# Rotary embedding: one GpSimd product per tile over a signed sine table, instead of two half products

## The chip, the cores and the metric

The kernel runs on one core of one Trainium2 chip. The metric is device time in microseconds (us) of one execution. All data is float32.

## The reference: what is computed

A rotary position embedding on `x` of shape (8, 2048, 8, 64): batch, position, head, head element. `cos` and `sin` have shape (2048, 32).

```python
x1 = x[..., : x.shape[-1] // 2]
x2 = x[..., x.shape[-1] // 2 :]
cos = cos[None, :, None, :]
sin = sin[None, :, None, :]
out1 = x1 * cos - x2 * sin
out2 = x1 * sin + x2 * cos
return np.concatenate([out1, out2], axis=-1)
```

Each row of 64 elements is two halves of 32. The output row is `x * (cos, cos)` plus the row with its halves exchanged times `(-sin, sin)`. Input and output are 33.55 MB each.

## The kernel before, in words

**Tiling.** The 2048 positions are split over 128 partitions, 16 positions to a partition. A batch is then 8192 elements per partition (16 positions x 8 heads x 64), 4 MB in all, and it has one buffer `xt` in SBUF. There are five of these (`NBUF`). The loop over the 8 batches cuts each into pieces: four of 2048 elements (4 positions), but in batch 0 the first piece, and in batch 7 the last, is cut into two of 1024. So there are 30 pieces of 2048 and 4 of 1024. `rotate` computes one piece in place in `xt`.

**Loads and stores.** Loads are issued on the SP queue (L67), the first five batches at once, the tables behind the first quarter of batch 0. Batches 5 to 7 are loaded after batches 0 to 2 have been stored, since they take over their buffers. Stores are issued on ScalarE's queue (L74). Batch 0 goes out in five parts and batch 7 in three (4096, 2048 and 2048 elements per partition), the others whole, each after its last piece.

**The three kinds of piece.** `t1` holds `x * cos`, `t2` the exchanged row times the signed sine.

- Kind A, 29 of the 34 pieces: GpSimd makes `t2` in two products (L121): the second halves of `t2` from the first halves of `x` times `sin_sb`, then the first halves of `t2` from the second halves of `x` times `nsin`, the negated sine. VectorE makes `t1` in one product against the cosine table in PSUM (L128) and adds both into `xt` (L135). Here `t1` is in PSUM, in a pool of one buffer.
- Kind B, the first pieces of batches 2, 4 and 5: GpSimd and VectorE make `t2` and `t1` as before, but the sum is made on TensorE, as two products with the identity (L140, L141), and ScalarE copies it from PSUM into `xt` (L142).
- Kind C, the first pieces of batches 1 and 3: VectorE makes both products (L128, L145), TensorE adds them with `eye` and `neye`, ScalarE copies (L161). GpSimd has no part.

`t2` of GpSimd rotates through three buffers (`t2_pool`). In kinds B and C, `t1`, and in C `t2` too, lie in `t1s_pool`, two buffers in SBUF.

**Order.** Almost every instruction is wrapped in `keep`, so each engine runs them in the order in which the program states them. The framework adds the semaphores. GpSimd runs its products piece after piece; a new product waits until a buffer of `t2` is free, that is, until the add three pieces earlier is done.

**Tables before the loop.** ScalarE makes `nsin` (L89), copies sine to PSUM (L90) and negates the identity (L91). VectorE copies cosine to PSUM (L92).

Of the kernel before, what the change touches and what calls it, by code (L numbers as in the profile page):

```python
# [9 lines left out]
@with_exitstack  # L10
def kernel(
    ctx: ExitStack,
    tc: tile.TileContext,
    x: bass.AP,
    cos: bass.AP,
    sin: bass.AP,
    out: bass.AP,
):
    nc = tc.nc
    keep = tc.keep_in_program_order  # L20
    f32 = mybir.dt.float32
    PSUM = bass.MemoryType.PSUM

    B, S, H, D = x.shape
    Dh = D // 2
    P = 128
    HD = H * D
    R = S // P
    ROW = R * HD
    UNIT = 4 * HD  # L30
    NBUF = 5
    C = 512
    last = B - 1

    xv = x.rearrange("b (q r) h d -> b q (r h d)", q=P)
    ov = out.rearrange("b (q r) h d -> b q (r h d)", q=P)
    cos_src = cos.rearrange("(q r) d -> q r d", q=P)
    sin_src = sin.rearrange("(q r) d -> q r d", q=P)

    const_pool = ctx.enter_context(tc.tile_pool(name="const", bufs=1))  # L40
    tab_pool = ctx.enter_context(tc.tile_pool(name="tab", bufs=1, space=PSUM))
    t1_pool = ctx.enter_context(tc.tile_pool(name="t1p", bufs=1, space=PSUM))
    o_pool = ctx.enter_context(tc.tile_pool(name="op", bufs=2, space=PSUM))
    t1s_pool = ctx.enter_context(tc.tile_pool(name="t1s", bufs=2))
    xpool = ctx.enter_context(tc.tile_pool(name="xpool", bufs=NBUF))
    t2_pool = ctx.enter_context(tc.tile_pool(name="t2p", bufs=3))

    cos_sb = const_pool.tile([P, R, Dh], f32, tag="cb")
    sin_sb = const_pool.tile([P, R, Dh], f32, tag="sb")
    nsin = const_pool.tile([P, R, Dh], f32, tag="ns")  # L50
    eye = const_pool.tile([P, P], f32, tag="eye")
    neye = const_pool.tile([P, P], f32, tag="neye")
    cos_ps = tab_pool.tile([P, R, Dh], f32, tag="cp")
    sin_ps = tab_pool.tile([P, R, Dh], f32, tag="sp")

    xts = {}

    def spans(sizes):
        lo = 0
        for n in sizes:  # L60
            yield lo, n
            lo += n

    def load(b):
        xt = xpool.tile([P, ROW], f32, tag="xt", name=f"xt{b}")
        for lo, n in spans([UNIT, UNIT, 2 * UNIT] if b == 0 else [ROW]):
            keep(nc.sync.dma_start(out=xt[:, lo : lo + n], in_=xv[b, :, lo : lo + n]))  # L67
            if b == 0 and lo == 0:
                keep(nc.sync.dma_start(out=cos_sb, in_=cos_src))  # L69
                keep(nc.sync.dma_start(out=sin_sb, in_=sin_src))  # L70
        xts[b] = xt

    def store(b, lo, n):
        keep(nc.scalar.dma_start(out=ov[b, :, lo : lo + n], in_=xts[b][:, lo : lo + n]))  # L74

    for b in range(NBUF):
        load(b)

    nc.gpsimd.memset(eye, 0.0)  # L79
    nc.gpsimd.affine_select(  # L80
        out=eye,
        in_=eye,
        compare_op=mybir.AluOpType.not_equal,
        fill=1.0,
        base=0,
        pattern=[[-1, P]],
        channel_multiplier=1,
    )
    keep(nc.scalar.mul(nsin, sin_sb, -1.0))  # L89
    keep(nc.scalar.copy(sin_ps, sin_sb))  # L90
    keep(nc.scalar.mul(neye, eye, -1.0))  # L91
    keep(nc.vector.tensor_copy(cos_ps, cos_sb))  # L92

    def rep(a, n):
        return dataclasses.replace(a, ap=[a.ap[0][:], a.ap[1][:], [0, n], a.ap[-1][:]])

    kinds = {}
    for b, kind in ((1, "C"), (2, "B"), (3, "C"), (4, "B"), (5, "B")):
        kinds[(b, 0)] = kind

    def rotate(b, lo, n):
        kind = kinds.get((b, lo), "A")
        xt = xts[b][:, lo : lo + n]
        r0 = lo // HD
        nr = n // HD
        xk = xt.rearrange("p (r k d) -> p r k d", r=nr, d=Dh)
        xu = xt.rearrange("p (g u d) -> p g u d", u=2, d=Dh)
        if kind == "A":
            t1 = t1_pool.tile([P, n], f32, tag="t1")
        else:  # L110
            t1 = t1s_pool.tile([P, n], f32, tag="t1s")
        if kind == "C":
            t2 = t1s_pool.tile([P, n], f32, tag="t1s")
        else:
            t2 = t2_pool.tile([P, n], f32, tag="t2")
        t1u = t1.rearrange("p (g u d) -> p g u d", u=2, d=Dh)
        t2u = t2.rearrange("p (g u d) -> p g u d", u=2, d=Dh)
        if kind != "C":
            for u, tab in ((1, sin_sb), (0, nsin)):
                keep(  # L120
                    nc.gpsimd.tensor_mul(  # L121
                        out=t2u[:, :, u, :].rearrange("p (r h) d -> p r h d", h=H),
                        in0=xu[:, :, 1 - u, :].rearrange("p (r h) d -> p r h d", h=H),
                        in1=rep(tab[:, r0 : r0 + nr, :], H),
                    )
                )
        keep(
            nc.vector.tensor_mul(  # L128
                out=t1.rearrange("p (r k d) -> p r k d", r=nr, d=Dh),
                in0=xk,  # L130
                in1=rep(cos_ps[:, r0 : r0 + nr, :], 2 * H),
            )
        )
        if kind == "A":
            keep(nc.vector.tensor_add(out=xt, in0=t1, in1=t2))  # L135
        elif kind == "B":
            for j in range(n // C):
                o = o_pool.tile([P, C], f32, tag="o")
                cs = slice(j * C, (j + 1) * C)
                nc.tensor.matmul(o, eye, t1[:, cs], start=True, stop=False)  # L140
                nc.tensor.matmul(o, eye, t2[:, cs], start=False, stop=True)  # L141
                keep(nc.scalar.copy(xt[:, cs], o))  # L142
        else:
            keep(
                nc.vector.tensor_mul(  # L145
                    out=t2.rearrange("p (r k d) -> p r k d", r=nr, d=Dh),
                    in0=xk,
                    in1=rep(sin_ps[:, r0 : r0 + nr, :], 2 * H),
                )
            )  # L150
            G = C // Dh
            for u in range(2):
                for j in range(n // 2 // C):
                    o = o_pool.tile([P, C], f32, tag="o")
                    gs = slice(j * G, (j + 1) * G)
                    nc.tensor.matmul(o, eye, t1u[:, gs, u, :], start=True, stop=False)  # L156
                    nc.tensor.matmul(  # L157
                        o, eye if u else neye, t2u[:, gs, 1 - u, :], start=False, stop=True
                    )
                    keep(  # L160
                        nc.scalar.copy(  # L161
                            xu[:, gs, u, :], o.rearrange("p (g d) -> p g d", d=Dh)
                        )
                    )

    def pieces(b):
        if b == 0:
            return [2 * HD, 2 * HD, UNIT, UNIT, UNIT]
        if b == last:
            return [UNIT, UNIT, UNIT, 2 * HD, 2 * HD]  # L170
        return [UNIT] * 4

    for b in range(B):
        done = 0
        outs = list(spans([2 * UNIT, UNIT, UNIT] if b == last else [ROW]))
        for lo, n in spans(pieces(b)):
            rotate(b, lo, n)
            done = lo + n
            while outs and sum(outs[0]) <= done:
                whole = outs.pop(0)  # L180
                if b == 0:
                    for part in spans([HD, HD, 2 * HD, UNIT, 2 * UNIT]):
                        store(b, *part)
                else:
                    store(b, *whole)
        if b + NBUF <= last:
            load(b + NBUF)
# [30 lines left out]
```

## Time and profile before

| | |
|---|---|
| median of 6 runs | 163.62 us (163.49 to 165.58) |
| the profiled execution | 163.56 us |
| its span, first to last instruction | 161.8 us |
| GpSimd (POOL) busy | 138.9 us, 86% |
| VectorE (DVE) busy | 140.1 us, 87% |
| TensorE (PE) busy | 45.5 us, 28% |
| ScalarE (ACT) busy | 14.4 us, 9% |
| read from HBM, written | 34.08 MB, 33.55 MB |
| mean rate of the DMA engines over the span | 418 GB/s |

The profile is one execution as the hardware profiler took it. Its page cuts the span into 40 equal slices; in the rows of an engine each digit is its busy share in tenths. A row of the trace's timeline has the start from the span's begin, the duration, the engine, the line of the kernel, the operation, and what is written and read, with `t` for every temporary, whichever pool it is from; in square brackets stands how long the engine had been idle and what ended that. The chain of waits is found from the last instruction backwards: at each step to what released it. Durations of GpSimd instructions overlap their neighbours by some hundredths of a us, so their cost is better taken from start to start.

### The profile page before, as it was taken

The numbers are of one execution on the slowest core, as the hardware profiler recorded it, in microseconds if no ns is written. First come the engines' busy times: TensorE is split into PE (matmuls) and PEld (weight loads), VectorE is DVE, ScalarE is ACT, GpSimd is POOL, SyncE is SP. The second block draws the span as 40 slices with busy tenths as digits, with TensorE's granted clock in tenths as the row PEclk, the third lists the DMA queues.
The fourth block names the chain that finished last, engine by engine and source line by source line (L and its number), as shares of the span: only waits on it lengthen the run. The fifth ranks groups of instructions, "written<-read, shape, count | busy, mean of one in ns | idle before, by whom it ended". The sixth has DMA issues, their size and how long they took to land.

```text
span 161.8 us, 470 instructions
## 1 busy us (share of the span) xinstructions
PE 45.5 (28%) x80; PEld 18.3 (11%) x80; DVE 140.1 (87%) x66; ACT 14.4 (9%) x24; POOL 138.9 (86%) x70
## 2 busy tenths in 40 slices
PE   0000000499008930894039802990000000000000
PEld 0000000143003400341014201430000000000000
DVE  0468999999999999999999999999999999999600
ACT  3300000013100410022001400130000000000000
POOL 1299999999999899999994999999999999996000
PEclk9999999999965997589857995699555555555555
DMA  5999999999998989998999999999999999999995
GB/s 192 407 442 473 471 413 413 413 421 438 438 470 348 462 357 454 429 478 389 429 470 397 438 456 405 446 446 407 438 446 413 438 454 405 446 446 405 417 407 213
DMA packets 3746, 67.65 MB, mean 418 GB/s; under 512 B 416, under 2 KB 416, under 8 KB 1056
## 3 DMA queue, kind: packets, MB, share of 16 engines
q1 hardware_dynamic: 1728, 34.08, 49.7%
q10 hardware_dynamic: 2016, 33.56, 48.3%
q14 instruction: 2, 0.02, 0.0%
HBM read 34.08 MB, written 33.55 MB: 418 GB/s over the span
## 4 chain that ended last, share of the span: by engine, by line
DVE 75%; POOL 9%; issue 6%; DMA 3%; SPq 0%; DVEq 0%; POOLq 0%
DVE t L128 40%; DVE xt L135 33%; POOL t L121 9%; DMA sin_sb<-in_sin_dram 3%; DVE t L145 3%; DVEq L135 0%; SPq L69 0%; SPq L67 0%; POOLq L121 0%
## 5 line engine op out<-in xcount | busy, mean ns | idle before, releaser
L121 POOL TENSOR_TENSOR t<-xt,sin_sb 128x1024 f32<-128x1024 f32 (+1 forms) x32 | 70.4, 2200 | 8.7 <-DMA sin_sb<-in_sin_dram 5.6
L128 DVE TENSOR_TENSOR t<-xt,cos_ps 128x2048 f32<-128x2048 f32 (+1 forms) x34 | 73.4, 2167 | 0.8
L121 POOL TENSOR_TENSOR t<-xt,nsin 128x1024 f32<-128x1024 f32 (+1 forms) x32 | 70.5, 2202 | 0.0
L135 DVE TENSOR_TENSOR xt<-t,t 128x2048 f32<-128x2048 f32 (+1 forms) x29 | 62.2, 2145 | 5.4 <-POOL t L121 2.5
L140 PE MATMUL o<-t,eye 128*128 128x512 f32 x24 | 15.5, 733 | 25.4 <-DVE t L128 25.4
L156 PE MATMUL o<-t,eye 128*128 128x512 f32 x16 | 11.4, 821 | 37.9 <-DVE t L128 37.9
L141 PE MATMUL o<-t,eye 128*128 128x512 f32 x24 | 14.6, 695 | 0.0
L142 ACT COPY xt<-o 128x512 f32<-128x512 f32 x12 | 7.0, 586 | 44.8 <-PE o L141 44.8
L140 PEld LDWEIGHTS o<-t,eye 128*128 128x128 f32 x24 | 5.5, 246 | 33.5 <-issue 33.5
L161 ACT COPY xt<-o 128x512 f32<-128x512 f32 x8 | 4.7, 586 | 44.8 <-DVE t L128 26.6
L156 PEld LDWEIGHTS o<-t,eye 128*128 128x128 f32 x16 | 3.8, 257 | 42.8 <-POOL t L121 30.5
L141 PEld LDWEIGHTS o<-t,eye 128*128 128x128 f32 x24 | 5.4, 227 | 7.4 <-issue 7.4
L92 DVE COPY cos_ps<-cos_sb 128x512 f32<-128x512 f32 x1 | 0.7, 695 | 6.1 <-DMA cos_sb<-in_cos_dram 6.1
L157 PE MATMUL o<-t,neye 128*128 128x512 f32 x8 | 5.4, 780 | 0.1
L145 DVE TENSOR_TENSOR t<-xt,sin_ps 128x2048 f32<-128x2048 f32 x2 | 4.6, 2282 | 0.0
L157 PE MATMUL o<-t,eye 128*128 128x512 f32 x8 | 4.1, 592 | 0.0
L157 PEld LDWEIGHTS o<-t,neye 128*128 128x128 f32 x8 | 2.0, 262 | 4.2 <-issue 4.2
L157 PEld LDWEIGHTS o<-t,eye 128*128 128x128 f32 x8 | 1.5, 190 | 1.9 <-issue 1.9
L89 ACT ACT_TABLE_LOAD x1 | 1.3, 1283 | 0.7 <-PEq L202 0.7
L89 ACT ACTIVATE nsin<-sin_sb 128x512 f32<-128x512 f32 x1 | 0.6, 630 | 4.8 <-DMA sin_sb<-in_sin_dram 4.8
L90 ACT COPY sin_ps<-sin_sb 128x512 f32<-128x512 f32 x1 | 0.6, 579 | 0.0
L79 POOL MEMSET eye<- 128x128 f32 x1 | 0.2, 204 | 0.3 <-POOLq L202 0.3
(6 smaller groups left out, 1.0 us busy)
## 6 DMA issues: line engine op xcount, KB each, us to landing
xt<-in_x_dram SPq DMA_DIRECT2D x7, 4096.0 KB, 27.4
out_dram<-xt ACTq DMA_DIRECT2D x6, 4096.0 KB, 33.3
out_dram<-xt ACTq DMA_DIRECT2D x2, 2048.0 KB, 24.3
out_dram<-xt ACTq DMA_DIRECT2D x3, 1024.0 KB, 11.1
xt<-in_x_dram SPq DMA_DIRECT2D x2, 1024.0 KB, 6.0
xt<-in_x_dram SPq DMA_DIRECT2D x1, 2048.0 KB, 11.4
out_dram<-xt ACTq DMA_DIRECT2D x2, 256.0 KB, 19.0
out_dram<-xt ACTq DMA_DIRECT2D x1, 512.0 KB, 32.6
```

The lines of the kernel that those rows point to most:

```text
L89: keep(nc.scalar.mul(nsin, sin_sb, -1.0))
L92: keep(nc.vector.tensor_copy(cos_ps, cos_sb))
L121: nc.gpsimd.tensor_mul(out=t2u[:, :, u, :].rearrange("p (r h) d -> p r h d", h=H), in0=xu[:, :, 1 - u, :].rearrange("p (r h) d -> p r h d" ...
L128: nc.vector.tensor_mul(out=t1.rearrange("p (r k d) -> p r k d", r=nr, d=Dh), in0=xk, in1=rep(cos_ps[:, r0 : r0 + nr, :], 2 * H),)
L135: keep(nc.vector.tensor_add(out=xt, in0=t1, in1=t2))
L140: nc.tensor.matmul(o, eye, t1[:, cs], start=True, stop=False)
L141: nc.tensor.matmul(o, eye, t2[:, cs], start=False, stop=True)
L142: keep(nc.scalar.copy(xt[:, cs], o))
L145: nc.vector.tensor_mul(out=t2.rearrange("p (r k d) -> p r k d", r=nr, d=Dh), in0=xk, in1=rep(sin_ps[:, r0 : r0 + nr, :], 2 * H),)
L156: nc.tensor.matmul(o, eye, t1u[:, gs, u, :], start=True, stop=False)
L157: nc.tensor.matmul(o, eye if u else neye, t2u[:, gs, 1 - u, :], start=False, stop=True)
L161: nc.scalar.copy(xu[:, gs, u, :], o.rearrange("p (g d) -> p g d", d=Dh))
```

## The change

GpSimd's two products per piece become one over the whole piece. Its input is `x` with the two halves of each row exchanged: the pattern `swapped` starts at element 32 of a row, steps back by 32 to the other half, and on by 64 to the next row. Its table `sgn` holds for each position a negated and a plain sine row side by side, read by `signed` once for each of the 8 heads. The output is the piece of `t2` in one run. `nsin` goes.

`sgn` is made on ScalarE with four instructions, for positions 0 to 3 and then 4 to 15, ahead of the copy of sine to PSUM. The sine and cosine tables in SBUF lose their own places and lie in the two buffers of `t1s_pool`, which the first piece of kind C takes over later.

```diff
-    cos_sb = const_pool.tile([P, R, Dh], f32, tag="cb")
-    sin_sb = const_pool.tile([P, R, Dh], f32, tag="sb")
-    nsin = const_pool.tile([P, R, Dh], f32, tag="ns")
+    cos_sb = t1s_pool.tile([P, R, Dh], f32, tag="t1s", name="cos_sb")
+    sin_sb = t1s_pool.tile([P, R, Dh], f32, tag="t1s", name="sin_sb")
+    sgn = const_pool.tile([P, R, 2, Dh], f32, tag="sg")
...
-    keep(nc.scalar.mul(nsin, sin_sb, -1.0))
+    for lo, hi in ((0, 4), (4, R)):
+        keep(nc.scalar.mul(sgn[:, lo:hi, 0, :], sin_sb[:, lo:hi, :], -1.0))
+        keep(nc.scalar.copy(sgn[:, lo:hi, 1, :], sin_sb[:, lo:hi, :]))
     keep(nc.scalar.copy(sin_ps, sin_sb))
     keep(nc.scalar.mul(neye, eye, -1.0))
     keep(nc.vector.tensor_copy(cos_ps, cos_sb))
...
+    def swapped(a, nr):
+        return dataclasses.replace(
+            a,
+            offset=a.offset + Dh,
+            ap=[a.ap[0][:], [HD, nr], [D, H], [-Dh, 2], [1, Dh]],
+        )
+
+    def signed(a, nr):
+        return dataclasses.replace(
+            a, ap=[a.ap[0][:], [D, nr], [0, H], [Dh, 2], [1, Dh]]
+        )
...
         if kind != "C":
-            for u, tab in ((1, sin_sb), (0, nsin)):
-                keep(
-                    nc.gpsimd.tensor_mul(
-                        out=t2u[:, :, u, :].rearrange("p (r h) d -> p r h d", h=H),
-                        in0=xu[:, :, 1 - u, :].rearrange("p (r h) d -> p r h d", h=H),
-                        in1=rep(tab[:, r0 : r0 + nr, :], H),
-                    )
+            keep(
+                nc.gpsimd.tensor_mul(
+                    out=t2.rearrange("p (r h u d) -> p r h u d", r=nr, h=H, u=2),
+                    in0=swapped(xt, nr),
+                    in1=signed(sgn[:, r0 : r0 + nr, :, :], nr),
                 )
+            )
```

## The prediction

> **What bounds the kernel now.** I read the page first for the share of each engine, then its DMA lines, then the chain that ended last, and then asked the trace for stretches of time near the end.
>
> The page gives three resources that are nearly full: VectorE (DVE) is busy 87% of the span, GpSimd (POOL) 86%, and the DMA engines almost all of it. The DMA lines of the page:
>
> ```profile
> DMA  5999999999998989998999999999999999999995
> GB/s 192 407 442 473 471 413 413 413 421 438 438 470 348 462 357 454 429 478 389 429 470 397 438 456 405 446 446 407 438 446 413 438 454 405 446 446 405 417 407 213
> q1 hardware_dynamic: 1728, 34.08, 49.7%
> q10 hardware_dynamic: 2016, 33.56, 48.3%
> ```
>
> q1 carries the loads and q10 the stores; together their packets take 98.0% of 16 engines' span. Only the first and the last slice are half empty. The stretches of the trace (columns: stretch, length, busy time of PE, PEld, DVE, ACT, POOL, clock, DMA share, GB/s) say the same of the end:
>
> ```profile
> 5.00:20.00 15.00, 0.00 (x0) 0.00 (x0) 11.44 (x8) 1.35 (x3) 13.07 (x8) 1.00 1.04 441
> 120.00:140.00 20.00, 0.00 (x0) 0.00 (x0) 19.35 (x9) 0.00 (x0) 20.00 (x10) 0.50 0.98 424
> 140.00:152.00 12.00, 0.00 (x0) 0.00 (x0) 11.48 (x8) 0.00 (x0) 8.25 (x6) 0.50 1.00 430
> 158.00:160.00 2.00, 0.00 (x0) 0.00 (x0) 0.00 (x0) 0.00 (x0) 0.00 (x0) 0.50 0.86 365
> 160.00:161.80 1.80, 0.00 (x0) 0.00 (x0) 0.00 (x0) 0.00 (x0) 0.00 (x0) 0.50 0.02 9
> ```
>
> The DMA share stays near 1.0 until 159 us, though the last arithmetic ends at 152.5. So the chain of waits, which puts the end down to VectorE, has to be read with care:
>
> ```profile
> DVE 75%; POOL 9%; issue 6%; DMA 3%; SPq 0%; DVEq 0%; POOLq 0%
> ```
>
> That chain follows the last store back to the add that released it. It does not show that this store then stood behind others. The timeline of ScalarE's queue shows the last store issued at 152.51, the DMA lines from there on give its time to landing, and the DMA lines from the start to 152.5 what the store queue had moved by then:
>
> ```profile
> 152.51 0.34 ACTq L74 DMA_DIRECT2D out_dram<-xt  x1
> ...
> out_dram<-xt ACTq DMA_DIRECT2D x1, 1024.0 KB, 8.3
> ...
> q10 hardware_dynamic: 1655, 30.52, 46.6%
> ```
>
> All stores are 33.56 MB and the last is 1.05 MB, so 32.51 MB were issued before it; 32.51 - 30.52 = 1.99 MB were still waiting, which is 4.7 us at 427 GB/s (67.65 MB over about 158.3 us in which packets moved). The same subtraction gives 3.1 MB at the store of 147.3, 3.0 MB at that of 142.6 and 2.95 MB at that of 133.0. The store queue is never dry in the last 30 us, and before that both queues hold work. My reading: transfers set the end, and VectorE and GpSimd run a few us ahead of what they must. The shortest landing of any 1 MB transfer in the trace is 4.7 us (the first load), so the last store could be issued about 8.3 - 4.7 = 3.6 us later before the end moves: an estimate.
>
> Below that bound, VectorE and GpSimd race each other. The timelines of both in the second half (start, duration):
>
> ```profile
> 102.20 2.34 POOL L121 TENSOR_TENSOR t<-xt,sin_sb 128x1024 f32<-128x1024 f32 x1
> 104.50 2.36 POOL L121 TENSOR_TENSOR t<-xt,nsin 128x1024 f32<-128x1024 f32 x1
> 106.80 2.36 POOL L121 TENSOR_TENSOR t<-xt,sin_sb 128x1024 f32<-128x1024 f32 x1
> ...
> 143.35 1.26 POOL L121 TENSOR_TENSOR t<-xt,sin_sb 128x512 f32<-128x512 f32 x1
> 144.56 1.26 POOL L121 TENSOR_TENSOR t<-xt,nsin 128x512 f32<-128x512 f32 x1
> ...
> 102.28 2.29 DVE L135 TENSOR_TENSOR xt<-t,t 128x2048 f32<-128x2048 f32 x1 [0.33 <-POOL t L121]
> 104.61 2.29 DVE L128 TENSOR_TENSOR t<-xt,cos_ps 128x2048 f32<-128x2048 f32 x1
> 107.00 2.29 DVE L135 TENSOR_TENSOR xt<-t,t 128x2048 f32<-128x2048 f32 x1
> ```
>
> Start to start, a GpSimd pair takes 4.57 to 4.60 us and a VectorE pair of an A tile 4.72 us. VectorE is the slower one there; over the whole kernel it waits only 2.5 us for GpSimd, in three places:
>
> ```profile
> DVE xt L135 <- POOL t L121: 2.5, 3, 1.3
> ```
>
> **What the Trainium skill says.** "GPSIMD Engine Reference", section 3.1, gives 4497 ns for a two-input fp32 GpSimd instruction of 2048 elements. The trace agrees with the rate: its pair, 2 x 1024 elements in runs of 32, takes 4.57 us, so runs of 32 cost no more than the page's figure. Section 7 of that page charges about 50% more for reads whose element step exceeds 8 bytes. The innermost step stays one element here, so I don't apply it; nothing in the trace tests a step that goes back. "SBUF — State Buffer", section "SBUF: two separate sides", says that engines and DMA cannot slow each other, and that GpSimd shares one port pair with VectorE instructions that have two SBUF inputs. Here each VectorE product takes its table from PSUM (L128, L145), and each add takes t1 from PSUM, so there is one SBUF input at most; the trace agrees, with VectorE's 2.29 us unvarying beside busy GpSimd. "DMA: Bandwidth & Descriptors", section "Where 436 GB/s comes from", gives 435 GB/s as the ceiling of the port side and 358 as that of HBM. The trace's 427 GB/s is past the second and near the first; at 435 the same bytes would need 155.5 us, 2.8 us less than now.
>
> **The change, part by part.**
>
> GpSimd's products. Of 64 instructions 32 go. Cost per instruction from start-to-start times: 1024 elements 2.28, 512 elements 1.21, so 2.09 ns an element and 0.14 us fixed. A product of 2048 elements is then 0.14 + 2048 x 0.00209 = 4.42 us, one of 1024 is 2.28. Saved: about 0.15 us in each of 28 whole tiles and 0.14 in each of 4 half tiles, 4.8 us of GpSimd time together. None of it lies on the transfers' path. On VectorE's path lie only the waits of 2.5 us, and the next limit there is VectorE's own 4.72 us per tile. The unknown is the read that goes back by 32 elements once in 64. The address pattern has the same three levels as the sine operand had before, so I take no extra cost: 4.42. The ends: 4.35, since the output is now one contiguous run and the fixed part cannot go below nothing by much, and 6.6 if the page's 50% applied anyway.
>
> The tables. One ScalarE product of 512 columns (0.63) becomes two products and two copies, of 128 and of 384 columns. The 128-column row (neye, 0.30) bounds the first two: between 0.15 and 0.30 each, I take 0.27. Sine lands at 6.8, so GpSimd starts at about 7.4 instead of 6.92, 0.45 later (0.25 to 0.6). It waits for both halves, where before its first product needed only sine itself. The second pair and sin_ps and neye end near 9.2 instead of 8.2; their first users are at 11.8 (third tile), 30.3 and about 34, so they are hidden.
>
> The start then goes: first tile's product ready at 7.4 + 2.28 = 9.7 (before 9.4), second 12.0 (12.0), third 16.4 (16.4), fourth 20.9 (20.97). VectorE's first two adds are late by up to 0.35, the third by nothing. Stores of those tiles are issued that much later, while the loads alone keep the DMA engines full (share 1.04 from 5 to 20 us). Cost nothing; uncovered it would be 0.35.
>
> The wait of 0.33 at 102.28 goes (two products sooner, 0.30). VectorE then ends at 152.2 instead of 152.5, GpSimd near 145.
>
> Cosine and sine in the t1s buffers. Their next users are the C products of batch 1 at 28.1 and 30.3; the last readers of the tables end by 9.2. No wait, nothing moved on any queue. The DMA lists and their order are unchanged.
>
> Sum: the transfers' path changes by 0 (down to -0.3 if the last store's earlier issue counts). The profiled execution is 163.56 with a span of 161.8, 1.76 outside it; its own time is 0.06 below the median of 163.62. I take 163.5.
>
> **The rivals.**
>
> Rival 1, the engines set the end after all. For it: the chain is 75% VectorE. Against: the 1.99 MB waiting. It would give 0.25 for VectorE's end (163.3), and at the very most all of the 2.5 us of waits for GpSimd (161.1); only the upper part is faster by 1%. The first two waits, 1.34 and 0.84, are at the start, where GpSimd begins later, so that part is hardly to be had.
>
> Rival 2, slower: reading backwards costs GpSimd extra. For it: no row of the trace has such a read, and GpSimd has little room. Decision point: GpSimd may end 2.9 us later (VectorE's last add ends 4.24 us after GpSimd's end, and must follow it by 1.35) plus 3.6 us of store slack, so 154.7; (154.7 - 7.4 - 0.3) / 30 tile equivalents = 4.90 us per product. Above 0.48 us extra a tile, 15 ns for each of 32 backward steps, the kernel slows by 30 us for each us. At 25 ns a step (an assumed size) a product takes 5.22, GpSimd ends at 164.3, the last add at 165.6, its store lands 4.7 later and the span ends 1.0 after that: 171.3, and 173.1 as a time. Against it: three-level patterns already run at the page's rate.
>
> Rival 3, GpSimd sees no saving, because the fixed part is not paid once but hidden in the pitch. Then nothing moves but the start: 163.6, same as before.
>
> **How the numbers follow.** Transfers set the end and little moves: 0.71 with rival 3 in it, own range 163.0 to 164.3. Rival 2: 0.22. Rival 1 with over 1% gain, or transfers that run nearer 435 GB/s: 0.07. About 1% is what a measurement of this kernel tells from no change. Faster 0.07, same 0.71, slower 0.22. The range goes from 162.0 to 168.5: it leaves out most of rival 1's upper part (0.06) and the part of rival 2 with over 20 ns a step (0.14).
>
> **What would show it.** Right: products at a pitch near 4.42 us, GpSimd starting near 7.4 and waiting more for VectorE, VectorE ending near 152.2, DMA share still 98%, and over 1.5 MB of stores waiting when the last is issued. Wrong: a product over 4.9 us with VectorE waiting for GpSimd in every tile (rival 2), or an end that moves with VectorE's last add by more than 0.3 us (rival 1).

## The result and the profile after

The changed kernel takes 164.70 us (median of 28 runs), the kernel before beside it 163.92 (63 runs). The ratio is 1.0038, 95% interval 1.0019 to 1.0056: slower by 0.6 us, small but clear of no change. The ratio is taken over the fast runs alone, here and in the table below; the medians of all runs lie 0.8 us apart. The forecast was 163.5 us, a little faster than before.

The profiled execution of the changed kernel is one of its longer ones, 165.66 us with a span of 163.7, so the lines below show the effect larger than the median has it. Its page, the DMA lines:

```profile
DMA  5999999999999899999999999999999999999991
GB/s 190 424 446 491 408 410 407 452 440 432 398 432 474 340 422 492 360 456 440 384 456 424 432 450 400 448 440 408 456 424 432 448 400 440 456 400 416 414 422 52
q1 hardware_dynamic: 1728, 34.08, 49.1%
q10 hardware_dynamic: 2016, 33.56, 48.0%
```

The transfers still fill the span up to its last slice. That last slice is where the time is: 52 GB/s. The stretches of the trace at the end (columns as in the prediction):

```profile
120.00:140.00 20.00, 0.00 (x0) 0.00 (x0) 19.35 (x9) 0.00 (x0) 20.00 (x6) 0.50 0.98 424
140.00:152.00 12.00, 0.00 (x0) 0.00 (x0) 11.48 (x8) 0.00 (x0) 7.55 (x3) 0.50 1.00 431
158.00:160.00 2.00, 0.00 (x0) 0.00 (x0) 0.00 (x0) 0.00 (x0) 0.00 (x0) 0.50 0.88 373
160.00:162.00 2.00, 0.00 (x0) 0.00 (x0) 0.00 (x0) 0.00 (x0) 0.00 (x0) 0.50 0.16 66
```

From 120 to 160 us the rates are those of before. Between 160 and 162 us a DMA share of 0.16 remains, two or three of sixteen engines; before, these 2 us had 0.02. The sixteen completion times of the last store say it too: before, all lie between 159.8 and 160.8 us; after, thirteen lie between 159.8 and 160.6, and three at 161.5, 162.8 and 162.8. So most DMA engines end when they ended before, and three of them late (taking one completion time for each engine).

The store queue was not waiting for VectorE. ScalarE's timeline, the DMA lines from the last store's issue on, and those up to it:

```profile
152.91 0.34 ACTq L74 DMA_DIRECT2D out_dram<-xt  x1
...
out_dram<-xt ACTq DMA_DIRECT2D x1, 1024.0 KB, 9.9
...
q10 hardware_dynamic: 1658, 30.57, 46.8%
```

Before that store 32.51 - 30.57 = 1.94 MB were waiting (before: 1.99).

On the engines themselves the change did what it says. The group of whole products, GpSimd's timeline from 98 us on, the add that had waited 0.33 us before, and the waits between the two:

```profile
L134 POOL TENSOR_TENSOR t<-xt,sgn 128x2048 f32<-128x2048 f32 x28 | 125.8, 4521 | 5.2 <-DVE xt L148 5.2
...
98.12 49.42 POOL L134 TENSOR_TENSOR t<-xt,sgn 128x2048 f32<-128x2048 f32 x12 [0.21 <-DVE xt L148]
...
102.68 2.29 DVE L148 TENSOR_TENSOR xt<-t,t 128x2048 f32<-128x2048 f32 x1 [0.23 <-POOL t L134]
...
POOL t L134 <- DVE xt L148: 5.2, 8, 2.3
DVE xt L148 <- POOL t L134: 2.5, 3, 1.7
```

Where neither waits, a whole product starts 4.46 to 4.51 us after the one before it, mostly 4.47 to 4.48 (two halves: 4.57 to 4.60). So about 0.10 us are saved, and GpSimd returns most of that by waiting longer for VectorE, 5.2 us instead of 2.7.

**Where it comes from.** Three places in the trace differ before the end. The first is the first store. The DMA lines of the stretch from 14.0 to 15.45 us, before and then after (queue, packets, MB, share):

```profile
q1 hardware_dynamic: 16, 0.52, 83.7%
q10 hardware_dynamic: 16, 0.03, 5.8%
```

```profile
q1 hardware_dynamic: 16, 0.52, 83.7%
q10 hardware_dynamic: 13, 0.03, 4.7%
```

Each of the sixteen engines moves one load row of 32 KB here, and behind it one store row of 2 KB; the next pair follows 1.29 us later. Before, all sixteen have a store row in this slot. After, three have none and start one slot later. The store was issued at 10.69 us before and at 10.98 after.

The second is the load of batch 4. The text ahead of the prediction counts it among five loads issued at once, but the trace has it much later. The SP queue's timeline, before and then after:

```profile
35.03 0.33 SPq L67 DMA_DIRECT2D xt<-in_x_dram  x1
```

```profile
35.72 0.33 SPq L67 DMA_DIRECT2D xt<-in_x_dram  x1
```

The last of the sixteen completions of the second store, which runs behind the first, comes at 35.01 us before and at 35.71 after. In every trace here but that without the work of the pieces, this load is issued 0.01 to 0.02 us after that moment. So the load takes over the lateness of the last engine, 0.7 us.

The third is the time in which loads start again beside stores of whole batches, from 60 to 80 us; before and then after:

```profile
60.00:80.00 20.00, 9.37 (x16) 3.67 (x16) 19.52 (x10) 2.34 (x4) 19.88 (x10) 0.83 1.04 446
```

```profile
60.00:80.00 20.00, 9.06 (x16) 3.64 (x16) 19.52 (x10) 2.34 (x4) 19.60 (x5) 0.81 1.03 433
```

13 GB/s less over 20 us are 0.26 MB, 0.6 us at the mean rate of 427 GB/s. That resembles the loss between the medians, but it does not account for this execution, whose span is 1.9 us longer. Over the whole stretch from 5 to 158 us the rates are 430 GB/s before and 429 after. What differs is how evenly the DMA engines run: the sixteen completion times of the load of batch 5 spread over 2.0 us before (85.9 to 88.0) and over 3.6 us after (85.9 to 89.5), and those of the last store over 1.0 and 3.0 us.

### The profile page after: what moved, and what is told of

It is laid out like the page before. It is cut to its first block, busy times and chain, and to the rows that moved or that the text cites. A ratio compares the mean times of both kernels' runs of the same rounds, so it can differ in the third digit from the quotient of the medians.

```text
span 163.7 us, 443 instructions
## 1 busy us (share of the span) xinstructions
PE 45.5 (28%) x80; PEld 18.4 (11%) x80; DVE 140.1 (86%) x66; ACT 15.0 (9%) x27; POOL 135.7 (83%) x38
## 4 chain that ended last, share of the span: by engine, by line
DVE 73%; POOL 8%; issue 8%; DMA 3%; SPq 0%; DVEq 0%; ACT 0%
DVE t L141 39%; DVE xt L148 31%; POOL t L134 8%; DMA sin_sb<-in_sin_dram 3%; DVE t L158 3%; DVEq L148 0%; SPq L69 0%; SPq L67 0%; ACT sgn L91 0%; ACT sgn L90 0%
## 5 line engine op out<-in xcount | busy, mean ns | idle before, releaser
L134 POOL TENSOR_TENSOR t<-xt,sgn 128x2048 f32<-128x2048 f32 (+1 forms) x32 | 135.0, 4249 | 11.2 <-ACT sgn L91 6.0
L90 ACT ACTIVATE sgn<-sin_sb 128x128 f32<-128x128 f32 (+1 forms) x2 | 0.8, 413 | 4.8 <-DMA sin_sb<-in_sin_dram 4.8
L91 ACT COPY sgn<-sin_sb 128x128 f32<-128x128 f32 (+1 forms) x2 | 0.8, 387 | 0.0
```

The lines of the kernel that those rows point to most:

```text
L90: keep(nc.scalar.mul(sgn[:, lo:hi, 0, :], sin_sb[:, lo:hi, :], -1.0))
L91: keep(nc.scalar.copy(sgn[:, lo:hi, 1, :], sin_sb[:, lo:hi, :]))
L134: nc.gpsimd.tensor_mul(out=t2.rearrange("p (r h u d) -> p r h u d", r=nr, h=H, u=2), in0=swapped(xt, nr), in1=signed(sgn[:, r0 : r0 + nr, ...
```

## The experiments

The theory, A: the late start of GpSimd shifts the first store by 0.3 us, some DMA engines take its first row one load row later, and the transfers run less well afterwards. Its rivals are B, VectorE's later end moves the end; C, the tiles' new places in SBUF; D, the merged product itself.

All runs in one table. The columns between the name and the ratio are read from the profile of one execution, whose time is given too: issue of the first store, how many of the sixteen engines have a store row between 14.0 and 15.45 us, issue of the load of batch 4, and the rate from 60 to 80 us. The first load lands at 5.4 to 5.7 us of these traces, so times of issue compare to about 0.3 us.

| kernel | first store, us | of 16 | load of batch 4, us | GB/s | profiled, us | ratio to before (95%) |
|---|---|---|---|---|---|---|
| before | 10.69 | 16 | 35.03 | 446 | 163.56 | 1 |
| changed | 10.98 | 13 | 35.72 | 433 | 165.66 | 1.0038 (1.0019 to 1.0056) |
| changed, again (e1) | 11.18 | 14 | 35.70 | 435 | 165.60 | 1.0099 (1.0064 to 1.0134) |
| new tables, two products (e2) | 11.45 | 5 | 36.19 | 433 | 164.96 | 1.0045 (1.0022 to 1.0067) |
| changed, early start (e4) | 10.83 | 16 | 35.16 | 442 | 163.69 | 1.0009 (0.9991 to 1.0027) |
| before, copy beside store (e5) | 10.80 | 16 | 35.12 | 444 | 163.46 | 0.9994 (0.9972 to 1.0016) |
| before, store held 0.3 us (e6) | 11.11 | 12 | 35.83 | 430 | 165.22 | 1.0045 (1.0021 to 1.0069) |
| before, store held 1.1 us (e7) | 11.91 | 0 | 36.04 | 433 | 164.64 | 1.0034 (1.0021 to 1.0047) |
| changed, store held 0.8 us (e8) | 12.09 | 0 | 36.09 | 429 | 164.09 | 1.0028 (1.0008 to 1.0047) |
| transfers only (e9) | 6.96 | - | 39.41 | 424 | 164.24 | 1.0014 (0.9998 to 1.0031) |
| changed, first add split (e10) | 10.57 | 16 | 35.09 | 443 | 164.25 | 0.9996 (0.9975 to 1.0017) |
| before, first add split (e11) | 10.21 | 16 (three of them their second) | 35.03 | 445 | 164.25 | 0.9992 (0.9973 to 1.0012) |
| before, VectorE late (e12) | 10.83 | 16 | 35.15 | 438 | 163.70 | 0.9999 (0.9977 to 1.0020) |

**The changed kernel again.** No edit.

> The changed kernel once more, beside the others on the same chip. If the loss of 0.4% belongs to the kernel, the ratio to the kernel before comes out near 1.004 (1.001 to 1.007) again. If it was the luck of the first measurement, near 1.000.

Measured 1.0099 (1.0064 to 1.0134), median 165.58 of 8 runs. The loss belongs to the kernel. Its size is not fixed: larger than in the first measurement and past the range expected.

**Which half of the change.** The new tables and places with the two half products:

```diff
-            keep(
-                nc.gpsimd.tensor_mul(
-                    out=t2.rearrange("p (r h u d) -> p r h u d", r=nr, h=H, u=2),
-                    in0=swapped(xt, nr),
-                    in1=signed(sgn[:, r0 : r0 + nr, :, :], nr),
-                )
-            )
+            for u in (1, 0):
+                tab = sgn[:, r0 : r0 + nr, u, :]
+                keep(
+                    nc.gpsimd.tensor_mul(
+                        out=t2u[:, :, u, :].rearrange("p (r h) d -> p r h d", h=H),
+                        in0=xu[:, :, 1 - u, :].rearrange("p (r h) d -> p r h d", h=H),
+                        in1=rep(tab, H),
+                    )
+                )
```

> The setup half of the change alone: sgn made as in the changed kernel, cosine and sine in the t1s buffers, GpSimd starting near 7.35 us, but two half products per piece, reading sgn. Theory A (the late start shifts the first stores by 0.3 us, and so the order in which loads and stores alternate on each DMA engine, and a few engines end later): near 1.004. Theory C (the places of the tiles in SBUF): near 1.004. Theory B (VectorE's later end moves the end): 1.002 to 1.004. Theory D (the merged product itself disturbs something): 1.000.

Measured 1.0045. The merged product is not needed for the loss, so D falls as its cause. The DMA lines from 14.0 to 15.45 us of this kernel show the slot missed by eleven engines:

```profile
q1 hardware_dynamic: 18, 0.56, 89.1%
q10 hardware_dynamic: 5, 0.01, 1.8%
```

The other half, the changed kernel with its first piece made as before:

```diff
+            if b == 0 and lo == 0:
+                for u, tab in ((1, sin_sb), (0, sgn[:, :, 0, :])):
+                    keep(
+                        nc.gpsimd.tensor_mul(
+                            out=t2u[:, :, u, :].rearrange("p (r h) d -> p r h d", h=H),
+                            in0=xu[:, :, 1 - u, :].rearrange(
+                                "p (r h) d -> p r h d", h=H
+                            ),
+                            in1=rep(tab[:, r0 : r0 + nr, :], H),
+                        )
+                    )
+            else:
...
```

> The changed kernel, but the first piece (1024 elements) is made in two half products, the first straight from the sine table as it lands, so that GpSimd starts near 6.9 us and the first store is issued near 10.7 us as before. Theory A: back to 1.000 (0.998 to 1.002). Theories C and D: still 1.004. Theory B: 1.000 to 1.002, with VectorE's end near 152.2 us.

Measured 1.0009 (0.9991 to 1.0027): the loss is gone, with the tiles where the change put them and 31 merged products of 32. So C falls, and D once more. VectorE's last add ends at 152.7 us here, not at 152.2, so B is not told apart by this run.

**The first store alone.** The kernel before with a copy on ScalarE ahead of the first store:

```diff
+                    for _ in range(1):
+                        o = o_pool.tile([P, C], f32, tag="o")
+                        keep(nc.scalar.copy(o[:, :128], xts[b][:, :128]))
                     for part in spans([HD, HD, 2 * HD, UNIT, 2 * UNIT]):
```

> The kernel before with one ScalarE copy of 128 columns (about 0.3 us) ahead of the first store of batch 0, so that this store is issued near 11.0 us instead of 10.7 and nothing else moves on GpSimd or VectorE. Theory A: 1.002 to 1.006, with the sixteen landings of the last store spread over 2 us or more. Theories B, C and D: 1.000.

Measured 0.9994, but the edit missed its aim. ScalarE's timeline:

```profile
10.80 0.27 ACT L184 COPY o<-xt 128x128 f32<-128x128 f32 x1 [2.54 <-DVE xt L135]
10.80 8.39 ACTq L74 DMA_DIRECT2D out_dram<-xt  x4
```

The store is issued as the copy starts: nothing made it wait. The run does not test A; it does show that such a copy on ScalarE costs nothing that can be measured. In the next one the copy goes from the piece onto itself, and the store has to wait for it:

```diff
+                    keep(nc.scalar.copy(xts[b][:, :128], xts[b][:, :128]))
                     for part in spans([HD, HD, 2 * HD, UNIT, 2 * UNIT]):
```

> The kernel before with one ScalarE copy of 128 columns of the first piece onto itself between its add and the first store; the store waits for it and is issued near 11.0 us, as in the changed kernel, while GpSimd and VectorE run as before and no tile moves. Theory A (the first store reaches the DMA engines on both sides of a boundary between two load rows): of the sixteen first store packets 1 to 8 are missing between 14.0 and 15.45 us, the last store's landings spread over 2 us or more, ratio 1.003 to 1.010. Theory B (VectorE's later end moves the end): 1.000. Theory C (places in SBUF): 1.000.

Measured 1.0045 (1.0021 to 1.0069). ScalarE's timeline, then the stretch from 14.0 to 15.45 us, then that from 60 to 80:

```profile
10.79 0.30 ACT L182 COPY xt<-xt 128x128 f32<-128x128 f32 x1 [2.54 <-DVE xt L135]
11.11 0.86 ACTq L74 DMA_DIRECT2D out_dram<-xt  x2
...
q1 hardware_dynamic: 16, 0.52, 83.7%
q10 hardware_dynamic: 12, 0.02, 4.3%
...
60.00:80.00 20.00, 9.53 (x16) 3.81 (x16) 19.52 (x10) 2.35 (x4) 19.89 (x10) 0.83 1.03 430
```

The first store, and the second behind it in the queue, are issued about 0.3 us later. Four engines come in the next slot, and the last store's completions spread from 159.9 to 162.5 us. GpSimd's products, the tables and all places are those of the kernel before. So holding the first store is enough for a loss of the change's size.

**Is it a boundary?** A longer hold on the kernel before (the diff), and one on the changed kernel, there with copies of 512 and 128 columns:

```diff
+                    keep(nc.scalar.copy(xts[b][:, :512], xts[b][:, :512]))
+                    keep(nc.scalar.copy(xts[b][:, :384], xts[b][:, :384]))
                     for part in spans([HD, HD, 2 * HD, UNIT, 2 * UNIT]):
```

> The kernel before with two such copies, of 512 and 384 columns: the first store is issued near 11.8 us, 1.1 us later than before. Theory A, as a boundary: all sixteen DMA engines now take the first store row one load row later, none between 14.0 and 15.45 us, they are in step again, and the ratio is back at 1.000 (0.998 to 1.003), below that of the run with 0.3 us. A theory in which any delay of the first store costs time: 1.005 or more. Theory B: 1.000.

> The changed kernel with two such copies, of 512 and 128 columns: the first store is issued near 11.8 us, 0.8 us later than in the changed kernel. Theory A, as a boundary: a further delay makes the changed kernel faster, 0.998 to 1.003 against 1.004 to 1.010 without it. Theories B and C: 1.004 or more, as VectorE's end and the places of the tiles stay what they are in the changed kernel.

Measured 1.0034 (1.0021 to 1.0047) and 1.0028 (1.0008 to 1.0047). The trace shows the boundary: none of the sixteen has a store row between 14.0 and 15.45 us, all sixteen in the next slot, and in the 1.1 us run that store lands within 25.3 to 25.7 us on all engines. The time does not follow as A had it: being in step again did not bring back the whole 0.4%. The stretch from 60 to 80 us of the 1.1 us run is slow, too:

```profile
60.00:80.00 20.00, 9.84 (x16) 3.94 (x16) 19.52 (x10) 2.35 (x4) 19.88 (x10) 0.68 1.03 433
```

But this is no loss over a longer stretch. From 40 to 80 us the run moves as much as the kernel before; before, then the 1.1 us run:

```profile
40.00:80.00 40.00, 18.56 (x33) 7.29 (x32) 39.10 (x18) 5.27 (x9) 39.32 (x18) 0.83 1.01 426
```

```profile
40.00:80.00 40.00, 20.16 (x35) 7.90 (x33) 39.10 (x18) 5.28 (x9) 39.38 (x18) 0.71 1.01 427
```

So the late store costs time whether some engines miss the slot or all of them, and the rate from 60 to 80 us does not measure it. Which part of the lateness costs is not shown. In every kernel with a loss the load of batch 4 is late as well, at 35.70 to 36.19 us against 35.03 to 35.16, and no run has a late store row without that late load. (The run without the pieces' work, e9 below, has the load at 39.41 us, but differs in too much else to tell.) Whether the further delay made the changed kernel faster is unclear: 1.0028 lies below 1.0099 of the same kernel without it, but beside 1.0038.

**What sets the end.** All work of the pieces left out, so that the loads are stored as they are:

```diff
         for lo, n in spans(pieces(b)):
-            rotate(b, lo, n)
             done = lo + n
```

> The kernel before with all the work of the pieces left out: only loads, tables and stores, each store waiting for its load alone. If transfers set the end, as the prediction said, this takes 160 to 164 us (0.98 to 1.00) although VectorE and GpSimd do nothing; if the engines set it, clearly less, near 157 us[...].

Measured 1.0014 (0.9998 to 1.0031). Without any product or add of the pieces, the same loads and stores take as long, though the last store is issued at 127.7 us. And VectorE 2.3 us later in batch 6, everything before it untouched:

```diff
-        keep(
+        for _ in range(2 if b == 6 and lo == 0 else 1):
+            keep(
...
```

> The kernel before with one cosine product of batch 6 made twice, so that VectorE ends about 2.3 us later and the last four stores are issued that much later, while nothing moves in the first 110 us. If transfers set the end and the last store has 3.6 us of slack, as the prediction said: 1.000 (0.998 to 1.002). If VectorE sets the end (theory B): 1.014.

Measured 0.9999 (0.9977 to 1.0020). VectorE's last line of the timeline:

```profile
153.72 1.22 DVE L136 TENSOR_TENSOR xt<-t,t 128x1024 f32<-128x1024 f32 x1
```

It ends at 154.9 us instead of 152.5, and the time stays. B falls.

**An early first store.** The first add cut in two, in the changed kernel and in the one before:

```diff
-            keep(nc.vector.tensor_add(out=xt, in0=t1, in1=t2))
+            cuts = [(0, HD), (HD, n)] if b == 0 and lo == 0 else [(0, n)]
+            for a, z in cuts:
+                keep(
+                    nc.vector.tensor_add(out=xt[:, a:z], in0=t1[:, a:z], in1=t2[:, a:z])
+                )
```

> The changed kernel with VectorE's first add cut in two halves of 512 elements, so that the first store can be issued near 10.4 us (before: 10.7; changed: 11.0). GpSimd's single products, the tables and the late start of GpSimd stay. Theory A: all sixteen first store packets lie between 14.0 and 15.45 us again, 60 to 80 us move 440 GB/s or more, ratio 0.997 to 1.002. Theory C (places in SBUF) and B (VectorE's end, which comes still a little later here): 1.004 or more.

> The kernel before with the same cut of the first add: first store near 10.15 us, further from the boundary near 10.9. Theory A: 0.997 to 1.001, with fewer runs above 164.3 us than the kernel before has. Theory B: 1.001, since VectorE has one more instruction.

Measured 0.9996 and 0.9992; neither differs from the kernel before by more than the interval. In the changed kernel the cut takes the loss away, as far as the ratios of two measurements can be compared (the changed kernel itself was not run beside it):

```profile
10.57 0.93 ACTq L74 DMA_DIRECT2D out_dram<-xt  x2
...
q1 hardware_dynamic: 16, 0.52, 83.7%
q10 hardware_dynamic: 16, 0.03, 5.8%
...
60.00:80.00 20.00, 9.97 (x16) 4.04 (x16) 19.52 (x10) 2.34 (x4) 19.60 (x5) 0.69 1.03 443
```

In the kernel before it brings nothing that can be measured. Of the cut's 14 runs one is above 164.3 us, of the 35 runs of before beside it seven are, too few to tell. Its trace has one thing more. Three engines take their first store row already at 13.6 to 13.8 us, a slot ahead of the other thirteen; the load of batch 4 is in time, and no loss shows. So disorder among the engines alone did not make a loss here. No version tried is faster than the kernel before.

## Why the prediction was right and where it was wrong

**The bound: right.** Transfers set the end. The transfers alone take 1.0014 of the time, and VectorE may end 2.5 us later for nothing. The 155.5 us at 435 GB/s were an estimate from a stated ceiling; the transfers alone, at 429 GB/s from 5 to 158 us, did not reach it. The chain of waits, with VectorE at 73% of it, misleads here as the prediction said.

**The slack of 3.6 us: right as far as tried,** 2.5 us of it.

**GpSimd's products: right in kind.** 4.42 us expected, 4.47 measured; the saving per tile is 0.10 us and not 0.15. Either two instructions made into one save less than the fixed part of the fit, or the step back by 32 elements costs these 0.05 us; no run separates the two. Rival 2 is out: a product is far below its decision point of 4.90.

**The tables: right.** GpSimd starts at 7.34 us (expected 7.4), the first two adds are 0.29 us late and the third 0.07.

**VectorE's end: wrong, without effect.** Expected 152.2, measured 152.9. The wait for GpSimd at 102 us did shrink, from 0.33 to 0.23. But at 90.5 us VectorE stands still for 0.5 us for which the trace names only its own preceding instruction, already ended. The runs e1, e2, e4 and e8 have such a wait of 0.5 us too, and so has e11, which is the kernel before with its first add cut; e10, with the whole change, has none. So it does not follow the change, and its cause is open.

**The start: the step that failed.** The prediction had: "Stores of those tiles are issued that much later, while the loads alone keep the DMA engines full (share 1.04 from 5 to 20 us). Cost nothing; uncovered it would be 0.35." The shift was seen and sized well, 0.29 us, and the engines are indeed full while it happens. The inference is what fails. Here the full queue hid the late store's own time, but the store's rows moved behind later load rows, and a load that waits for the second store moved with them. The prediction had nothing of either. The held store alone gives 1.0045, and the early first piece takes the loss out of the changed kernel (1.0009, where the changed kernel run beside it has 1.0099). The term for this step was 0 and measured 0.6 us.

**What stays open:** how a first store that comes one load row later at 14 us makes some DMA engines end late at 160. The trace has steps between, the late load of batch 4 and, in the changed kernel, the wide spread of batch 5's load (3.6 us; in e7 and e8 only 0.5 and 0.3), but no run shows that one brings on the next. The mean rate says little of it: from 5 to 158 us it is 429 to 431 GB/s in all thirteen traces. The size is not pinned down either, as the two measurements of the changed kernel, 0.4% and 1.0%, show.

## What to carry to other kernels

In this kernel the DMA engines are full from start to end. Work on the compute engines gained nothing, and a small shift in the setup cost time by where it put the first store between two load rows. Where that may be so elsewhere, look at two things before a setup step is priced at nothing: how near the first store's issue is to such a boundary (count its packets in the slot), and which loads wait for the landing of an early store. When a copy is meant to delay a store, make the store depend on it.

## What the runs showed that was not expected

- With both queues busy, each DMA engine alternates load row and store row: one 32 KB row and one 2 KB row in 1.29 us. Counted from the landing of the first load, a first store issued 5.0 to 5.3 us later had its first row in this slot on all sixteen engines (before, e4, e5, e10, e12), one issued 5.6 us later on 12 to 14 (changed, e1, e6), at 5.7 on five (e2), at 6.4 and 6.5 on none (e7, e8).
- The loads of the first five batches were not issued at once: in the kernel before, that of batch 3 came at 14.18 us and that of batch 4 at 35.03, right behind the landing of the second store.
- A delay of about 0.3 us on two 256 KB stores, 150 us before the end, cost 0.7 us (1.0045), about twice the delay.
- ScalarE's queue issued a store at 10.80 us, at the moment a copy queued before it started (e5).
- A GpSimd product over 2048 elements, with a read that steps back by 32 elements in every row of 64, took 4.47 us start to start, less than two products of 1024 without such a step (4.57 to 4.60).
